# Transposing the inner activations of MLP and FFN: by TensorE, or by VectorE in 32 x 32 blocks with DMAs between partitions

## The chip, the cores and the metric

The kernel runs on one core of one Trainium2 chip. The metric is the device time of one execution in microseconds, lower is better; times of several runs are given as a median with the lowest and the highest.

The engines are named as in the profile: PE is TensorE, the matrix engine; PEld its weight loads; DVE is VectorE; ACT is ScalarE; POOL is GpSimd; SP is SyncE, whose queue issues DMAs here. An on-chip tile lies in SBUF on 128 partitions; PE writes its results to PSUM.

## What is computed

Two transformer blocks run over 256 tokens of width 1024, all in float32. The first block has four layers, each with a mixer (retention, conformer convolution, short convolution) and a squared-ReLU MLP. The second block has two layers, each with a SwiGLU FFN, a token mixing of three branches, another FFN and a gated projection (PLE). The change touches the MLPs, four of them, and the FFNs, also four:

```python
def squared_relu_mlp(x, w1, w2):
    return jnp.square(jax.nn.relu(x @ w1)) @ w2      # 1024 -> 4096 -> 1024

def _swiglu(x, w1, w3, w2):
    return (jax.nn.silu(x @ w1) * (x @ w3)) @ w2     # 1024 -> 2816 -> 1024
```

The inner activation is the argument of the second product. It comes out of the first with the tokens on the partitions, and the second needs it with the inner features on the partitions: it has to be transposed in between.

## The kernel before

**Halves.** The 256 tokens are two halves of 128. Each half is a Python generator (`first`, `second`), and `drive` (line 267) steps them in turn over one stream of weights: in each step half 0 uses unit i of the stream and half 1 unit i - 4 (`PACE`, lag 4 in the phases "1" and "A", where the MLPs and the FFNs run).

**Units.** A unit is 128 x 1024 float32 of weights (512 KB). `plan_mlp` (406) cuts an MLP into 8 groups of 512 inner features: four units of `w1`, then four of `w2`. `plan_ffn` (803) cuts an FFN into 11 groups of 256 inner features: four units "f1", each half of w1 and half of w3 and therefore loaded by two DMAs, then two units "f2". In both the first product of group g + 1 comes before the second product of group g.

**The supply.** `fill` (255) runs ahead of the step: `load_unit` (182) issues the DMA of a unit on SP into one of five raw tiles (line 189), up to eight units ahead, and `split_unit` (192) makes two tiles of it, the weights rounded to float32r by ACT (`wh`, line 204) and the remainder by DVE (`whl`, line 205), up to two units ahead, into one of eight slots. A raw tile is free when line 205 has read it; a slot is free when half 1 has used the unit (`release`, 211).

**The products.** `mm3` (306) multiplies the rounded activation with both weight tiles and the activation's remainder with the rounded weights: three matmuls for each 512 columns, so 6 for a unit and half, 12 for a unit.

**The activation.** In `mlp` (422) the first product ends in a PSUM bank; ACT applies the ReLU (434), DVE squares it (436), and the tile goes into `r[g]`. Two units later, before the second unit of the second product of the group before (`k == 1`), `tr_split` (337) transposes it: four 128 x 128 transposes on PE into a PSUM bank (`tr`, 331, recorded at line 66), and `split` (322) makes the rounded tile `t2h` by ACT (327) and the remainder `t2l` by DVE (328). These are the left-hand sides of the second product's matmuls. For group 0 that stands just ahead of its second product. In `ffn` (821) it is the same with silu (833), the product with the other half (835), tiles of 256 columns and two transposes.

**Tiles.** `B2` (109) takes a tile from one of two rings of the phase, 2 KB and 1 KB for each partition; `RINGS` gives their lengths: 30 and 6 in phase "1" (the first block), 20 and 6 in phase "A" (the FFNs). MLP tiles come from the 2 KB ring, FFN tiles of 256 columns from the 1 KB ring.

**Order.** The kernel states data dependences through tiles, and a scheduler fixes each engine's order of instructions when the program is built; waits are semaphores. Each engine and each DMA queue then works in that order.

Of the kernel before, what the change touches and what calls it, by code (L numbers as in the profile page):

```python
# [19 lines left out]
# (lag of the second half in units, splits ahead, loads ahead)  # L20
PACE = {"1": (4, 2, 8), "A": (4, 2, 8), "M": (0, 3, 6), "B": (2, 1, 6), "P": (6, 1, 8)}
# taps of the conformer's convolution that go to TensorE
# [3 lines left out]
# 2 KB slots, 1 KB slots  # L26
RM = (42, 20)
RINGS = {"1": (30, 6), "A": (20, 6), "M": RM}
# [10 lines left out]
# sets of columns of w_in, a bank each; rwkv's low ranks come with the gated delta rule's a, b and GLA's low rank  # L39
# [11 lines left out]
class Builder:  # L51
# [39 lines left out]
    # ---- phases: what fills the on-chip memory  # L91
# [16 lines left out]
    # ---- tiles  # L108
# [11 lines left out]
    def any(s, tag, shape):  # L120
        """outside the projections all four banks serve alike"""
        if s.kind == "M":
            s.turn = not s.turn
            tag = "mm" if s.turn else "tp"
        return s.bank(tag, 2, shape)
# [18 lines left out]
    def rows(s, keep, name, *vecs):  # L144
        """vectors of 128 n entries as n rows each of one tile"""
        n = sum(v.shape[0] for v in vecs)
        t = s.const.tile([n, 128], F32, tag="p " + name, name=name) if keep else s.B2((n, 128), name)
        o = 0
        for v in vecs:
            s.pin(s.nc.gpsimd.dma_start(t[o:o + v.shape[0]], v))  # L150
            o += v.shape[0]
        return t

    def columns(s, name, *rows):
        """those rows as columns"""
        n = sum(r.shape[0] for r in rows)
        t = (s.pool if s.kind == "1" else s.const).tile([128, n], F32, tag="p " + name, name=name)
        tp = s.tpb((128, n))
        o = 0
        for r in rows:  # L160
            k = r.shape[0]
            s.nc.tensor.transpose(tp[:, o:o + k], r, s.ident[0:k, 0:k])
            o += k
        s.nc.vector.tensor_copy(t, tp)
        return t

    # ---- weight stream
# [24 lines left out]
    def split_unit(s, i, early):  # L192
        """the weights as a float32r tile and the float32r rest"""
        nc = s.nc
        r, n = s.r[i], s.width[i]
        if s.plan[i][0] in EXACT:
            s.w[i] = r
            return True
        tag = s.take(s.whq, early)
        if tag is None:  # L200
            return False
        s.slot[i][1] = tag
        wh, wl = s.tile_of(tag, F32R), s.tile_of(tag, F32R, "l")
        nc.scalar.copy(wh[:, 0:n], r[:, 0:n])  # L204
        nc.vector.tensor_tensor(wl[:, 0:n], r[:, 0:n], wh[:, 0:n].bitcast(F32), op=ALU.subtract)  # L205
        s.w[i] = (wh, wl)
        s.rawq.append(s.slot[i][0])
        s.slot[i][0] = None
        return True
# [9 lines left out]
    def side_step(s, wait=True):  # L219
        """one step of the mixing that is next in turn, has what it needs and whose last step is LATENCY past"""  # L220
# [21 lines left out]
    def side_run(s):  # L242
        """what goes beside half a unit"""
# [11 lines left out]
    def fill(s, u, ahead, load, stop):  # L255
        """loads and splits that run ahead of unit u; what is for another phase takes no slot of this one's"""
# [48 lines left out]
    # ---- pieces  # L305
# [16 lines left out]
    def split(s, src):  # L322
# [4 lines left out]
        nc.scalar.copy(hh, src)  # L327
        nc.vector.tensor_tensor(ll, src, hh.bitcast(F32), op=ALU.subtract)  # L328
# [7 lines left out]

    def tr_split(s, src):
        return s.split(s.tr(src))

    def linear(s, lhs, KT, name, n=1024, out=None):  # L340
        """units of [128 K, 1024 columns]; yields the two banks"""
# [11 lines left out]
    def rstd(s, v, r=None):  # L353
        """v [128, n] already holds mean square + eps"""
# [19 lines left out]
    def times(s, x, g):  # L374
        """x g, the start of rms_norm(x, g); the scale per token is left to what follows the product"""
# [6 lines left out]
    def pre_lhs(s, x, y):  # L382
        """that transposed and split, and the scale"""
# [5 lines left out]
    def post_rms(s, ps, x, g, after):  # L389
        """x + rms_norm(ps, g), and that times the vector after"""  # L390
# [14 lines left out]
    # ---- MLP  # L405
# [16 lines left out]
    def mlp(s, h, lhs, rin):  # L422
# [4 lines left out]
        def w1(g):  # L427
# [9 lines left out]
            r[g] = a2  # L437

        yield from w1(0)
        for g in range(8):  # L440
            if g < 7:
                yield from w1(g + 1)
            at = nxt if g else [s.tr_split(r.pop(g))]
            for k in range(4):
                W = yield "w2"
                if g < 7 and k == 1:
                    nxt = [s.tr_split(r.pop(g + 1))]
# [3 lines left out]
    # ---- retention  # L451
    def ret_consts(s):
# [9 lines left out]
        for h in range(2):  # L462
# [19 lines left out]
            # columns: cos | cos | -sin | sin  # L482
# [16 lines left out]
    def rotary(s, h, ps, rin):  # L499
        """ps: two banks of 2 heads x (t1 128 | t2 128); returns transposed [128 d, 8, 128 tok] as two tiles"""  # L500
# [84 lines left out]
    # ---- conformer conv  # L585
# [23 lines left out]
    def depthwise(s, c, raws):  # L609
        """gate and convolution of channels 256 c .. 256 c + 255, both halves; DVE and TensorE share the taps"""  # L610
# [89 lines left out]
    # ---- short conv  # L700
# [51 lines left out]
    # ---- first block  # L752
# [9 lines left out]
    def layer_vec(s, key, vec, norm=False):  # L762
        """a replicated vector, loaded by the first half that asks"""
# [38 lines left out]
    # ---- second block: SwiGLU, LayerNorm, PLE  # L802
# [18 lines left out]
    def ffn(s, h, lhs):  # L821
# [4 lines left out]
        def w1(g):  # L826
# [9 lines left out]
            r[g] = b  # L836

        yield from w1(0)
        for g in range(11):
            if g < 10:  # L840
                yield from w1(g + 1)
            at = nxt if g else [s.split(s.tr(r.pop(g), 2)[:, 0:2, :])]
            for k in range(2):
                W = yield "f2"
                if g < 10 and k == 1:
                    nxt = [s.split(s.tr(r.pop(g + 1), 2)[:, 0:2, :])]
# [3 lines left out]
    def lhs(s, src, exact):  # L850
        """transposed: as it is or split"""
# [7 lines left out]
    def post_ln(s, ps, w, x, g, b):  # L859
        """x = layer_norm(alpha * x + w * ps), taken as that of x + w / alpha * ps"""  # L860
# [42 lines left out]
    # ---- second block: token mixing  # L903
# [15 lines left out]
    def mix_load(s, i):  # L919
        """the mixers' parameters of a layer, and what is fixed"""  # L920
# [76 lines left out]
    def token_mix(s, h, lhs, i):  # L997
# [7 lines left out]
        for name, cols in SETS:  # L1005
# [7 lines left out]
            if name.startswith("gate"):  # L1013
                # sigmoid(z) = (1 + tanh(z / 2)) / 2, the last half left to the end
# [19 lines left out]
    def weave(s, main, beside):  # L1034
        """main, with a step of the other after each of its own"""
# [7 lines left out]
    def inverse(s, nb, Lq, Lx, D=None):  # L1043
        """inverses of I + L (of 1 / D + L) for strictly lower triangular 64 x 64 blocks L, two above each other in each
        of nb columns of blocks; Lq(m, q) is the transposed q-th 32 x 32 diagonal block of column m, Lx(m, e) the
        transposed lower left 32 x 32 block; returns the transposed inverses, [128, nb, 64]"""
# [67 lines left out]
    def rwkv(s, h, i, q):  # L1114
# [39 lines left out]
        # sigmoid(z) = (1 + tanh(z / 2)) / 2, the halves left to what follows  # L1154
# [22 lines left out]
        # cumulative log decay inside chunks of 64, over -exp(-1/2) / 2  # L1177
# [18 lines left out]
        # kk, 2 a * kk  # L1196
# [9 lines left out]
        # decayed: [128 channels of two heads, pair, chunk (a | r), token]  # L1206
# [22 lines left out]
        def beside():  # L1229
            """what the state will need, while the inverses are on their way"""  # L1230
# [11 lines left out]
            for c in range(2):  # L1242
# [7 lines left out]
                if c == 0:  # L1250
# [5 lines left out]
                    # values, the tokens of two heads on the partitions  # L1256
# [111 lines left out]
    def softplus(s, x, w):  # L1368
        """max(x, 0) + ln(1 + exp(-|x|))"""
# [9 lines left out]
    def gdn(s, h, i, q):  # L1379
# [29 lines left out]
        # k and q side by side, two heads a tile  # L1409
# [16 lines left out]
        # columns of ss: k 0-3, q 4-7  # L1426
# [10 lines left out]
        # ln(beta / (k.k + eps))  # L1437
# [38 lines left out]
        def beside():  # L1476
            if h:
                # keys of the first half
# [41 lines left out]
        # the second chunk of 64 after the first  # L1520
# [23 lines left out]
        # rq = (q.q + eps)^-1/2 / sqrt(dk); rms over rq * O  # L1544
# [26 lines left out]
    def gla(s, h, i, q):  # L1571
# [21 lines left out]
        for b in range(2):  # L1593
            # -(z + b)
# [6 lines left out]
        # cumulative sums of -16 log a over the half  # L1601
# [9 lines left out]
        def score(kx, qx, out, n=128, keys=(0,), queries=(0,)):  # L1611
            """scores of blocks of n keys and n queries that begin at these; out(e, bank, j-th block)"""
# [15 lines left out]
        def scaled(sz):  # L1628
            """keys of the first half of each block of 2 sz, queries of the second"""
# [203 lines left out]
```

## Time and profile before

| what | us |
|---|---|
| time, median of 3 runs | 3053.36 (3052.99 to 3053.74) |
| span of the profiled execution, first to last instruction | 3051.7 |
| PE busy | 2964.7 |
| DVE busy | 1927.7 |
| ACT busy | 1521.7 |

The profile is of one execution; its page gives the span and no separate time, and it stands 1.7 us below the median of the timed runs. The mean granted clock of PE in it is 0.992.

In the rows of instruction groups the columns are line, engine, operation, output <- input with their shapes, count, then busy time in us, mean ns of one, and the idle time of the engine just before them with what ended most of it. In timelines the columns are start and duration in us, engine, line, operation, tile and count. In rows of waits they are who waited, for whom, us in total, times, longest. In rows of DMA issues they are output <- input, queue, count, KB each, and median us from issue to landing. In the rows of one tile's instructions the durations are the least, the median and the greatest in ns.

### The profile page before, as it was taken

What the parts mean: (1) busy time and instruction counts of PE and PEld (TensorE: products, weight loads), DVE (VectorE), ACT (ScalarE), POOL (GpSimd) and SP (SyncE); (2) the same over time, 40 slices, a digit from 0 to 9 for tenths busy, and PEclk for the clock granted to TensorE, in tenths of its full rate; (3) what the DMA queues carried; (4) which work ended last, traced back from release to release, by engine and by line L of the source; (5) the groups of instructions that cost most, each with busy time, mean ns of one, the idle gap of its engine ahead of it and who ended that gap; (6) DMA issues with size and microseconds to landing.
All of it is one profiled execution on the core that took longest, in us unless ns stands there. A gap on an engine that the chain in (4) does not pass through costs nothing. (4 is left out here: it accounts for less than half of the span.)

```text
span 3051.7 us, 48503 instructions
## 1 busy us (share of the span) xinstructions
PE 2964.7 (97%) x19034; PEld 2370.0 (78%) x19034; DVE 1927.7 (63%) x3039; ACT 1521.7 (50%) x2348; POOL 216.9 (7%) x349
## 2 busy tenths in 40 slices
PE   7999998999999999999999999999999999999998
PEld 5777876787878777787887787778878788777786
DVE  6566569656665666655556857565575576567556
ACT  4345454544554544544446566544444386644443
POOL 1000025000000000200000000000020000000000
PEclk9999999999999999999999999999999999999999
DMA  7456652455566655665664333466566543335663
GB/s 236 152 175 189 183 166 83 145 181 186 178 189 183 192 162 161 202 185 177 186 186 141 92 111 107 137 202 188 181 208 188 146 147 91 106 116 170 196 188 123
DMA packets 256325, 498.52 MB, mean 163 GB/s; under 512 B 24917, under 2 KB 125473, under 8 KB 256096
## 3 DMA queue, kind: packets, MB, share of 16 engines
q1 hardware_dynamic: 247424, 470.82, 50.5%
q0 software_dynamic: 8096, 22.49, 2.6%
q8 instruction: 150, 2.46, 0.3%
q10 hardware_dynamic: 576, 2.10, 0.2%
q14 instruction: 79, 0.65, 0.1%
HBM read 494.28 MB, written 1.05 MB: 162 GB/s over the span
## 5 line engine op out<-in xcount | busy, mean ns | idle before, releaser
L59 PE MATMUL acc<-wh,t2h 128*128 128x512 f32 (+1 forms) x1736 | 714.6, 413 | 16.7 <-ACT t2h L327 16.3
L205 DVE TENSOR_TENSOR whl<-raw,wh 128x1024 fp32r<-128x1024 f32 (+1 forms) x400 | 484.5, 1214 | 344.7 <-ACT wh L204 343.7
L59 PE MATMUL acc<-whl,t2h 128*128 128x512 f32 (+1 forms) x1736 | 682.6, 394 | 0.0
L204 ACT CAST wh<-raw 128x1024 fp32r<-128x1024 f32 (+1 forms) x400 | 415.8, 1042 | 459.5 <-PE acc L59 319.3
L59 PE MATMUL acc<-wh,t2l 128*128 128x512 f32 (+1 forms) x1736 | 594.4, 394 | 1.7 <-DVE t2l L328 1.6
L59 PEld LDWEIGHTS acc<-wh,t2h 128*128 128x128 f32 x1736 | 328.1, 189 | 98.1 <-ACT t2h L327 23.7
L59 PEld LDWEIGHTS acc<-wh,t2l 128*128 128x128 f32 x1736 | 326.9, 189 | 77.8 <-DVE t2l L328 5.5
L205 DVE TENSOR_TENSOR whxl<-raw,whx 128x1024 fp32r<-128x1024 f32 x213 | 260.2, 1223 | 195.9 <-ACT whx L204 195.9
L59 PEld LDWEIGHTS acc<-whl,t2h 128*128 128x128 f32 x1736 | 328.8, 189 | 62.2 <-issue 1.8
L204 ACT CAST whx<-raw 128x1024 fp32r<-128x1024 f32 x213 | 222.6, 1049 | 213.9 <-PE mm L59 130.2
L59 PE MATMUL mm<-whx,t2h 128*128 128x512 f32 x800 | 315.2, 394 | 0.6 <-ACT t2h L327 0.6
L59 PE MATMUL mm<-whx,t2l 128*128 128x512 f32 x800 | 314.4, 393 | 0.7 <-DVE t2l L328 0.7
L59 PE MATMUL mm<-whxl,t2h 128*128 128x512 f32 x800 | 313.8, 392 | 0.0
L205 DVE TENSOR_TENSOR whl<-rawx,wh 128x1024 fp32r<-128x1024 f32 x142 | 173.7, 1225 | 140.0 <-ACT wh L204 139.7
L205 DVE TENSOR_TENSOR whxl<-rawx,whx 128x1024 fp32r<-128x1024 f32 x145 | 177.1, 1222 | 129.2 <-ACT whx L204 129.2
L59 PE MATMUL acc<-whx,t2h 128*128 128x512 f32 x632 | 256.6, 406 | 1.1 <-ACT t2h L327 1.1
L59 PE MATMUL acc<-whxl,t2h 128*128 128x512 f32 x632 | 250.5, 396 | 0.0
L204 ACT CAST whx<-rawx 128x1024 fp32r<-128x1024 f32 x145 | 151.7, 1048 | 151.4 <-PE mm L59 101.4
L204 ACT CAST wh<-rawx 128x1024 fp32r<-128x1024 f32 x142 | 149.1, 1050 | 140.8 <-PE acc L59 97.2
L59 PE MATMUL acc<-whx,t2l 128*128 128x512 f32 x632 | 201.4, 395 | 0.3 <-DVE t2l L328 0.3
L327 ACT CAST t2h<-tp 128x512 fp32r<-128x512 f32 (+1 forms) x232 | 116.1, 504 | 131.1 <-PE tp L66 103.4
L59 PEld LDWEIGHTS mm<-whx,t2l 128*128 128x128 f32 x800 | 149.9, 187 | 35.3 <-DVE t2l L328 1.1
(612 smaller groups left out, 4089.7 us busy)
## 6 DMA issues: line engine op xcount, KB each, us to landing
raw<-in_mlp_w SPq DMA_DIRECT2D x153, 512.0 KB, 3.7
raw<-in_w_in SPq DMA_DIRECT2D x128, 512.0 KB, 3.6
raw<-in_ffn_w SPq DMA_DIRECT2D x222, 256.0 KB, 3.1
rawx<-in_mlp_w SPq DMA_DIRECT2D x103, 512.0 KB, 3.7
rawx<-in_ffn_w SPq DMA_DIRECT2D x130, 256.0 KB, 3.1
raw<-in_ret_w_in SPq DMA_DIRECT2D x58, 512.0 KB, 4.3
raw<-in_ffn_w SPq DMA_DIRECT2D x50, 512.0 KB, 3.7
rawx<-in_ret_w_in SPq DMA_DIRECT2D x38, 512.0 KB, 4.4
```

What stands on the lines that cost most here:

```text
L59: r = m0(out, a, b, **k)
L204: nc.scalar.copy(wh[:, 0:n], r[:, 0:n])
L205: nc.vector.tensor_tensor(wl[:, 0:n], r[:, 0:n], wh[:, 0:n].bitcast(F32), op=ALU.subtract)
L327: nc.scalar.copy(hh, src)
```

## The change

`tr_dma` takes the place of the transposes. DVE's 32 x 32 block transpose turns each block of a [128 tokens, n x 128 features] tile in place, so that block (b, c, a), of token block b and feature block a of column c, holds its features on the partitions of token block b. Sixteen DMAs then carry, for each pair (a, b), the blocks from partitions 32 b to 32 a of a second tile. A DMA moves 32 partitions with n x 32 contiguous floats each: 512 bytes in the MLP (n = 4), 256 bytes in the FFN (n = 2). They are issued on SP.

They are called where the activation is made, right after line 436 or 835, and no longer at `k == 1`; there only the split stays, and it reads `ty` in SBUF through a rearranged view, not a PSUM bank. The 1 KB ring of phase "A" grows from 6 to 12 tiles. Other transposes (the inputs of the blocks, of PLE and of the mixers) stay on PE. Comments and docstrings are removed as well.

```diff
-RINGS = {"1": (30, 6), "A": (20, 6), "M": RM}
+RINGS = {"1": (30, 6), "A": (20, 12), "M": RM}
...
     def split(s, src):
...
-        nc.scalar.copy(hh, src)
-        nc.vector.tensor_tensor(ll, src, hh.bitcast(F32), op=ALU.subtract)
+        cut = (lambda t: t.rearrange("p c (b j) -> p c b j", j=32)) if len(src.shape) == 4 else (lambda t: t)
+        nc.scalar.copy(cut(hh), src)
+        nc.vector.tensor_tensor(cut(ll), src, cut(hh.bitcast(F32)), op=ALU.subtract)
         return hh, ll
...
+    def tr_dma(s, src, n):
+        nc = s.nc
+        z = s.B2((128, 4, n, 32), "tz")
+        nc.vector.transpose(z, src.rearrange("p (c a j) -> p a c j", a=4, j=32))
+        y = s.B2((128, 4, n, 32), "ty")
+        for a in range(4):
+            for b in range(4):
+                nc.sync.dma_start(y[32 * a:32 * a + 32, b], z[32 * b:32 * b + 32, a])
+        return y.rearrange("p b c j -> p c b j")
...
     def mlp(s, h, lhs, rin):
...
-            r[g] = a2
+            r[g] = s.tr_dma(a2, 4)
...
-            at = nxt if g else [s.tr_split(r.pop(g))]
+            at = nxt if g else [s.split(r.pop(g))]
...
-                    nxt = [s.tr_split(r.pop(g + 1))]
+                    nxt = [s.split(r.pop(g + 1))]
...
     def ffn(s, h, lhs):
...
-            r[g] = b
+            r[g] = s.tr_dma(b, 2)
...
-            at = nxt if g else [s.split(s.tr(r.pop(g), 2)[:, 0:2, :])]
+            at = nxt if g else [s.split(r.pop(g))]
...
-                    nxt = [s.split(s.tr(r.pop(g + 1), 2)[:, 0:2, :])]
+                    nxt = [s.split(r.pop(g + 1))]
```

## The prediction

> **What bounds the kernel now.** I read the page's head first, then the idle times in its fifth part, then the timeline around the transposes that go, and last the queue that is to carry the new transfers.
>
> ```profile
> span 3051.7 us, 48503 instructions
> PE 2964.7 (97%) x19034; PEld 2370.0 (78%) x19034; DVE 1927.7 (63%) x3039; ACT 1521.7 (50%) x2348; POOL 216.9 (7%) x349
> L59 PE MATMUL acc<-wh,t2h 128*128 128x512 f32 (+1 forms) x1736 | 714.6, 413 | 16.7 <-ACT t2h L327 16.3
> L204 ACT CAST wh<-raw 128x1024 fp32r<-128x1024 f32 (+1 forms) x400 | 415.8, 1042 | 459.5 <-PE acc L59 319.3
> L205 DVE TENSOR_TENSOR whl<-raw,wh 128x1024 fp32r<-128x1024 f32 (+1 forms) x400 | 484.5, 1214 | 344.7 <-ACT wh L204 343.7
> SPq L189 <- DVE whl L205: 1213.8, 414, 25.4
> ```
>
> PE is busy 97% of the span, and its largest group waited only 16.7 us in the whole run. The supply chain waits backwards: the cast L204 waits for PE to give a weight tile back, the subtraction L205 waits for the cast, and the load queue (SPq) waits 1213.8 us for that subtraction to free a raw tile. So TensorE sets the pace, and whatever leaves its queue in the MLP and the FFN shortens the span, as long as the supply keeps up.
>
> **What goes.** A modelled duration is not what a transpose costs, since matmuls overlap; the starts show it.
>
> ```profile
> L66 PE MATMUL tp<-ident,relu x256: 270/272/273, 249.1 to 1422.1; 128*128 128x128 f32 x128
> 702.29 0.40 PE L59 MATMUL mm<-whx,t2l 128*128 128x512 f32 x1
> 702.52 0.60 PE L66 MATMUL tp<-ident,relu 128*128 128x128 f32 x4
> 702.88 0.48 PE L59 MATMUL acc<-wh,t2h 128*128 128x512 f32 x1
> 703.20 0.39 PE L59 MATMUL acc<-whl,t2h 128*128 128x512 f32 x1
> ...
> L66 PE MATMUL tp<-ident,glu x176: 270/271/272, 1455.3 to 3008.9; 128*128 128x128 f32 x176
> 1505.94 0.39 PE L59 MATMUL mm<-wh,t2l 128*128 128x512 f32 x1
> 1506.18 0.38 PE L66 MATMUL tp<-ident,glu 128*128 128x128 f32 x2
> 1506.31 0.48 PE L59 MATMUL acc<-whx,t2h 128*128 128x512 f32 x1
> 1506.63 0.39 PE L59 MATMUL acc<-whxl,t2h 128*128 128x512 f32 x1
> ```
>
> A matmul starts every 0.23 us. From 702.29 to 703.20 are 0.91 us, where two steps would take 0.46: four transposes cost 0.45 us. From 1505.94 to 1506.63 are 0.69 us: two cost 0.22 (with 0.232 for a step). That is 256/4 x 0.445 = 28.5 us in four MLPs and 176/2 x 0.22 = 19.4 us in four FFNs, 47.9 us in all.
>
> **What comes on VectorE and ScalarE.** The first half's tile is transposed by a STREAM_TRANSPOSE, which the kernel has elsewhere:
>
> ```profile
> L1078 DVE STREAM_TRANSPOSE invTT<-invT 128x256 f32<-128x256 f32 x20 | 8.8, 439 | 0.2
> L1078 DVE STREAM_TRANSPOSE invTT<-invT 128x128 f32<-128x128 f32 x20 | 6.2, 309 | 0.6
> L327 ACT CAST t2h<-tp 128x512 fp32r<-128x512 f32 x144 | 83.4, 586 | 101.3 <-PE tp L66 99.9 <-PE acc L59 0.7
> L327 ACT CAST t2h<-hoT 128x512 fp32r<-128x512 f32 x8 | 4.5, 616 | 0.0
> L327 ACT CAST t2h<-tp 128x256 fp32r<-128x256 f32 x88 | 32.6, 371 | 29.8 <-PE acc L59 26.3 <-PE tp L66 3.5
> L328 DVE TENSOR_TENSOR t2l<-tp,t2h 128x256 fp32r<-128x256 f32 x88 | 37.0, 420 | 9.8 <-ACT t2h L327 9.8
> ```
>
> 128 more columns cost 130 ns, so 512 take about 0.70 us. 64 x 0.70 + 88 x 0.44 = 84 us on a VectorE that is 63% busy: hidden behind matmuls. The split reads SBUF where it read PSUM: 616 ns for hoT, which lies in SBUF, is near the 586 ns of the PSUM form. Reading in runs of 32 has no row; between no change and a doubling it stays under PE's cover, and I take no change. The larger ring costs no time.
>
> **What comes on the load queue.** This is the term that decides. Each activation tile becomes 16 DMAs, and there are 64 + 88 tiles: 2432 issues, 1408 of them in the FFNs, all on SP, which also issues the weight loads in order. No row has a DMA of 32 partitions within SBUF; the nearest are SP's own loads:
>
> ```profile
> 722.63 0.33 SPq L189 DMA_DIRECT2D raw<-in_mlp_w  x1
> 759.60 0.80 SPq L189 DMA_DIRECT2D rawx<-in_sc_w_in  x2
> 1513.04 0.88 SPq L189 DMA_DIRECT2D rawx<-in_ffn_w  x2
> 1602.87 1.40 SPq L189 DMA_DIRECT2D raw<-in_w_in  x3
> L189 SPq DMA_DIRECT2D rawx<-in_ffn_w x168: 328/368/1217, 1435.1 to 2981.8; - x168
> ...
> raw<-in_ffn_w SPq DMA_DIRECT2D x222, 256.0 KB, 3.1
> raw<-in_w_in SPq DMA_DIRECT2D x8, 8.0 KB, 2.7
> raw<-in_w_in SPq DMA_DIRECT2D x8, 16.0 KB, 2.5
> ```
>
> An issue that had a wait ahead takes 0.33 us. One right behind another adds 0.80 - 0.33 = 0.47 (128 rows, one piece each). In pairs of 256 pieces it adds 0.88 - 0.37 = 0.51. In the group of three, where the second and third move only 8 and 16 KB, it adds (1.40 - 0.37)/2 = 0.51 as well: bytes do not count. From 128 to 256 pieces it grows by 0.04, so 32 pieces take off 0.03: 0.44. The ends are 0.33 and 0.51; I take **0.45**, nearest to the 0.47 row. One tile then occupies SP for 16 x 0.45 = 7.2 us.
>
> A group of the MLP (8 weight units, two halves of the tokens) needs 14.4 us of new issues and 8 loads at about 0.40, 17.6 us, against 8 x 12 x 0.232 = 22.3 us of matmuls: PE still sets the pace, and the 28.5 us come free. A group of the FFN has 6 units, four of them loaded by two DMAs:
>
> ```profile
> 1455.32 0.38 PE L66 MATMUL tp<-ident,glu 128*128 128x128 f32 x2
> 1472.53 0.38 PE L66 MATMUL tp<-ident,glu 128*128 128x128 f32 x2
> ```
>
> Its period is 17.2 us now. Its issues are 14.4 + 4 x (0.37 + 0.05 + 0.51) + 2 x 0.38 = 18.9 us: SP becomes the bound. Per FFN: 352 x 0.45 = 158.4, pairs 44 x 0.93 = 40.9, single loads 22 x 0.38 = 8.4, together 207.7 us. To this comes what SP cannot overlap: 3.1 us at the start (the first four units of one half, silu, product and transpose take 6.8 us, during which SP issues four pairs, 3.7), and 6.3 us after the last issue (landing 2.7, cast 0.37, subtraction 0.42, two units of one half 2.8). Five units stand loaded when the stage begins: -4.7. Result 212.4 us, against 11 x 17.2 = 189.3 us: **+23.1 us** per FFN, +92.4 for four. The 19.4 us of removed transposes are inside that and gain nothing.
>
> Behind a waiting issue on SP stand the weight loads, and behind a split that waits for its tile stand the casts on ScalarE. In the MLP both have cover: an activation is used some 20 us after it is made (the second product of the group before and the first of the one after, 8 units of 2.8 us, stand between), while transpose, issues, landing and split take 0.7 + 7.2 + 2.5 + 1.3 = 11.7. Only the last group of a stage has no further first-product group in between. At the FFN's end the cover is almost nothing:
>
> ```profile
> 1620.89 0.40 DVE L835 TENSOR_TENSOR glu<-silu,mm 128x256 f32<-128x256 f32 x1
> 1622.86 0.39 PE L59 MATMUL acc<-wh,t2h 128*128 128x512 f32 x1
> ```
>
> 1.6 us from the product's end to its use; that tail is in the 6.3 us above. At the MLP's end four units of 1.4 us (alone) to 2.8 us (beside the other half) stand against 11.7: 0.6 to 6.1 us are bare. I take 2 per MLP, +8 in all, since the other half mostly runs beside.
>
> **Sum:** -28.5 + 8 + 92.4 = +71.9 us on a span of 3051.7: 3123.6. The median shown is 3053.36, so 1.7 us lie around the span: **3125 us**.
>
> The DMA engines themselves are no bound:
>
> ```profile
> 205.00:400.00 195.00, 194.03 (x874) 156.50 (x874) 110.39 (x116) 94.20 (x117) 8.57 (x14) 1.00 0.62 185
> ```
>
> The last two columns are their busy share and GB/s in an MLP; a group moves 0.5 MB more in 22 us, 24 GB/s beside 185.
>
> The Trainium skill, page "DMA: Bandwidth & Descriptors", section "Rules for kernel authors", speaks against the change too, by another reason: it wants small transfers coalesced, since under 64 KB one pays mostly overhead. These are 16 and 8 KB, and the 8 KB row above lands after 2.7 us where the 256 KB loads take 3.1; the trace agrees, but by the sum it is the issue and not the landing that costs.
>
> **The rivals.**
>
> *Faster: the issues are cheap or hide.* If a 32-partition DMA costs 0.38 us (0.33 and the 0.05 between two), an FFN needs 352 x 0.38 + 49.3 (the loads) + 4.7 (both ends) = 187.8 us, 1.5 less than now: 3051.7 - 6.0 - 20.5 + 1.7 = 3026.9. With all tails covered too the whole 47.9 us come: 3005.5. It decides below 0.40 us per issue, where the FFNs lose less than the MLPs' 20.5 us. For it: the 0.33 of an issue that waited, and fewer pieces. Against: three rows of back-to-back issues at 0.47 and 0.51, whatever the bytes. The same page, section "Issuing engines are not separate DMA queues", says that the time an issue takes is usually small beside the transfer itself; by that rule the change would end at this rival's 3005.5. The trace has 0.47 beside 3.1 us for one load, which agrees for a single transfer and leaves out that 16 stand in a row.
>
> *Much slower: SP runs dry behind its own order.* After a tile's 16 issues comes the landing (2.7), the split's cast (0.37), and only then the cast and subtraction of a weight unit (1.04 + 1.21) that frees a raw tile: 5.3 us. If the order on ScalarE leaves only two units of loads to issue meanwhile (1.9), SP idles 3.4 us per tile, 88 x 3.4 = 300 us: 3425; at half of that, 3275. For it: casts and splits share one in-order queue. Against: the split of a tile stands two units behind its making, and raw tiles are loaded well ahead; the queue's waits for a landing are few:
>
> ```profile
> SPq L189 <- DMA rawx<-in_ffn_w: 5.6, 5, 2.5
> ```
>
> The upper end of the issue's price, 0.51, gives 352 x 0.06 x 4 = 84 us more: 3209.
>
> *No difference:* a price of 0.40 balances both, 3053.
>
> **How the numbers follow.** The forecast's kind, SP as the FFN's bound with a price of 0.41 to 0.51 and little extra idling: 0.58, from 3069 (at 0.41) to 3209 (at 0.51). Faster: 0.20. Within 0.2% (6 us, about what a measurement of this kernel can tell from no change): 0.05. SP running dry: 0.17. Slower in all 0.58 + 0.17 = 0.75. The range runs from 3015, which leaves out the lower part of the faster case, to 3280, which takes in half of the idling; about 0.08 and 0.11 stay outside.
>
> **What would show it.** Right: SP's issues of the new tiles stand 0.44 to 0.48 us apart; FFN groups come every 19 us or more, with PE waiting for weights or for the split, and MLP groups every 22.3 us; VectorE's transposes near 0.70 and 0.44 us with no one waiting for them. Wrong: issues under 0.40 us apart (the faster case); SP idle between tiles for landings or for VectorE, while PE waits (the dry case); or MLP groups over 23 us, which would mean that the split holds up the casts there as well.

## The result and the profile after

| kernel | median us | lowest to highest | runs |
|---|---|---|---|
| before | 3053.18 | 3052.49 to 3053.74 | 4 |
| after | 3744.95 | 3739.55 to 3748.74 | 4 |

The ratio is 1.226, 95% interval 1.2249 to 1.2278: the change costs 692 us, where the prediction had 72. First the head and three groups of the page of after.

```profile
span 3737.7 us, 51515 instructions
PE 3146.2 (84%) x18602; PEld 2434.9 (65%) x18602; DVE 2006.5 (54%) x3191; ACT 1528.3 (41%) x2348; POOL 216.2 (6%) x349
L59 PE MATMUL acc<-wh,t2h 128*128 128x512 f32 (+1 forms) x1736 | 727.3, 425 | 164.1 <-ACT t2h L328 152.9
L329 DVE TENSOR_TENSOR t2l<-ty,t2h 128x256 fp32r<-128x256 f32 (+1 forms) x152 | 81.6, 537 | 692.5 <-ACT t2h L328 672.8
L328 ACT CAST t2h<-ty 128x256 fp32r<-128x256 f32 (+1 forms) x152 | 75.1, 494 | 813.8 <-DMA ty<-tz 813.8
```

PE fell from 97% of the span to 84%. The casts of the carried tiles (L328) did not become slower themselves, but ScalarE sat idle 813.8 us ahead of them, always until the tile's DMAs had landed. The group that had waited 16.7 us now waits 164.1. PE no longer sets the pace in the MLP and the FFN. Two other views show what does. The waits of SP's queue, in a stretch of an MLP (970 to 1150 us) and then of an FFN (1720 to 1900 us); columns are who waited, for whom, us in total, times, longest:

```profile
SPq L347 <- DVE tz L343: 21.0, 10, 4.0
SPq L347 <- DMA raw<-in_mlp_w: 2.4, 3, 1.1
SPq L347 <- DMA rawx<-in_mlp_w: 1.4, 3, 0.8
```

```profile
SPq L347 <- DMA raw<-in_ffn_w: 4.7, 15, 0.7
SPq L347 <- DMA rawx<-in_ffn_w: 0.9, 4, 0.3
```

Before, SP spent most of an FFN waiting: 85.8 us of the 176 from 1455 to 1631 us for the subtraction L205 alone, and 48.1 for the activation's remainder (L328) and product (L835). In the FFN stretch of after it waits 5.6 of 180 us for loads to land and 2.3 for all else: it issues almost without a pause. The timeline of SP in an FFN shows one group of it (start and duration in us, then engine, line, operation, tile, count):

```profile
1803.67 10.01 SPq L347 DMA_DIRECT2D ty<-tz  x16
1813.78 0.53 SPq L189 DMA_DIRECT2D raw<-in_ffn_w  x1
1814.41 1.92 SPq L189 DMA_DIRECT2D rawx<-in_ffn_w  x4
1816.42 0.93 SPq L189 DMA_DIRECT2D raw<-in_ffn_w  x2
1817.45 10.69 SPq L347 DMA_DIRECT2D ty<-tz  x16
1828.25 1.55 SPq L189 DMA_DIRECT2D raw<-in_ffn_w  x3
1829.91 0.51 SPq L347 DMA_DIRECT2D ty<-tz  x1
```

From 1803.67 to 1829.91 are 26.2 us for two tiles and the ten loads of a group. Before, one half's SiLUs came 16.8 us apart through most of the stage (the 17.2 of the prediction is one of the first groups). A batch of 16 takes 10.0 us without a stop, 0.63 for each issue and not 0.45; the rest is the loads. In the MLP there are pauses. One tile there, on ScalarE, VectorE and SP (three timelines of the same stretch, in this order):

```profile
1048.84 0.62 ACT L328 CAST t2h<-ty 128x512 fp32r<-128x512 f32 x1 [7.12 <-DMA ty<-tz]
1049.36 0.68 ACT L447 ACTIVATE relu<-mm,rin 128x512 f32<-128x512 f32 x1
...
1063.11 0.62 ACT L328 CAST t2h<-ty 128x512 fp32r<-128x512 f32 x1 [6.43 <-DMA ty<-tz]
```

```profile
1050.10 0.68 DVE L449 TENSOR_TENSOR relu<-relu 128x512 f32<-128x512 f32 x1
1050.82 0.71 DVE L343 STREAM_TRANSPOSE tz<-relu 128x512 f32<-128x512 f32 x1
```

```profile
1051.59 10.01 SPq L347 DMA_DIRECT2D ty<-tz  x16
1061.70 0.53 SPq L189 DMA_DIRECT2D rawx<-in_mlp_w  x1
1062.32 1.36 SPq L189 DMA_DIRECT2D raw<-in_mlp_w  x3
1065.86 1.15 SPq L347 DMA_DIRECT2D ty<-tz  x2
```

Read them as one chain: the cast of one half's tile (1048.84), and only behind it, since ScalarE works in order, the ReLU of the other half (1049.36); the square, the block transpose, sixteen issues (to 1061.60), the landing, and the next cast at 1063.11. That is 14.3 us for a tile, 28.5 for a group. Over this stage one half's ReLUs come 29.1 us apart at the median; before it was 23.1.

Where the 686 us between the two spans lie is read from the starts of the ReLUs and SiLUs; each row has 16 or 22 of them, a stage, with the first and the last start at the end (before, after; MLP, then FFN):

```profile
L434 ACT ACTIVATE relu<-mm,rin x16: 689/690/692, 857.3 to 1020.5; 128x512 f32<-128x512 f32 x16
L833 ACT ACTIVATE silu<-mm x22: 378/384/386, 1444.1 to 1620.1; 128x256 f32<-128x256 f32 x22
```

```profile
L447 ACT ACTIVATE relu<-mm,rin x16: 681/682/690, 968.7 to 1180.6; 128x512 f32<-128x512 f32 x16
L846 ACT ACTIVATE silu<-mm x22: 373/377/384, 1667.6 to 1948.8; 128x256 f32<-128x256 f32 x22
```

An MLP's stage went from 163.2 to 211.9 us, an FFN's from 175.9 to 281.2. Summed in this way over the trace, the four MLP stages grew by 198.5 us and the four FFN stages by 419.8; the stretches behind the MLPs, up to the next stage's first such row or the end, grew by 26.1 and those behind the FFNs by 42.9; the stretch before the first lost 1.3. Together 686.0.

### The profile page after: what moved, and what is told of

It is laid out like the page before. It is cut to its first block, busy times and chain, and to the rows that moved or that the text cites. A ratio compares the mean times of both kernels' runs of the same rounds, so it can differ in the third digit from the quotient of the medians.

```text
span 3737.7 us, 51515 instructions
## 1 busy us (share of the span) xinstructions
PE 3146.2 (84%) x18602; PEld 2434.9 (65%) x18602; DVE 2006.5 (54%) x3191; ACT 1528.3 (41%) x2348; POOL 216.2 (6%) x349
## 5 line engine op out<-in xcount | busy, mean ns | idle before, releaser
L59 PE MATMUL acc<-wh,t2h 128*128 128x512 f32 (+1 forms) x1736 | 727.3, 425 | 164.1 <-ACT t2h L328 152.9
L205 DVE TENSOR_TENSOR whl<-raw,wh 128x1024 fp32r<-128x1024 f32 (+1 forms) x400 | 484.2, 1213 | 349.5 <-ACT wh L204 342.8
L59 PE MATMUL acc<-wh,t2l 128*128 128x512 f32 (+1 forms) x1736 | 612.3, 403 | 1.5 <-DVE t2l L329 1.4
L59 PEld LDWEIGHTS acc<-wh,t2h 128*128 128x128 f32 x1736 | 342.1, 198 | 271.1 <-ACT t2h L328 176.3
L329 DVE TENSOR_TENSOR t2l<-ty,t2h 128x256 fp32r<-128x256 f32 (+1 forms) x152 | 81.6, 537 | 692.5 <-ACT t2h L328 672.8
L59 PE MATMUL mm<-whx,t2h 128*128 128x512 f32 x800 | 341.0, 432 | 124.4 <-ACT whx L204 78.9
L59 PE MATMUL acc<-whx,t2h 128*128 128x512 f32 x632 | 281.1, 446 | 190.1 <-ACT t2h L328 171.8
L328 ACT CAST t2h<-ty 128x256 fp32r<-128x256 f32 (+1 forms) x152 | 75.1, 494 | 813.8 <-DMA ty<-tz 813.8
L205 DVE TENSOR_TENSOR whxl<-raw,whx 128x1024 fp32r<-128x1024 f32 x213 | 259.6, 1220 | 179.6 <-ACT whx L204 177.3
L59 PE MATMUL mm<-whxl,t2h 128*128 128x512 f32 x800 | 333.5, 422 | 2.5 <-DVE whxl L205 1.2
L59 PE MATMUL mm<-whx,t2l 128*128 128x512 f32 x800 | 329.1, 411 | 0.6 <-DVE t2l L329 0.6
L59 PEld LDWEIGHTS acc<-whx,t2h 128*128 128x128 f32 x632 | 131.7, 209 | 239.7 <-ACT t2h L328 191.5
L59 PEld LDWEIGHTS mm<-whx,t2h 128*128 128x128 f32 x800 | 160.1, 204 | 187.6 <-ACT whx L204 97.5
L59 PE MATMUL acc<-whxl,t2h 128*128 128x512 f32 x632 | 271.3, 430 | 0.1
L205 DVE TENSOR_TENSOR whxl<-rawx,whx 128x1024 fp32r<-128x1024 f32 x145 | 176.9, 1221 | 147.9 <-ACT whx L204 145.5
L205 DVE TENSOR_TENSOR whl<-rawx,wh 128x1024 fp32r<-128x1024 f32 x142 | 173.3, 1221 | 107.8 <-ACT wh L204 102.2
```

The lines of the kernel that those rows point to most:

```text
L59: r = m0(out, a, b, **k)
L328: nc.scalar.copy(cut(hh), src)
L329: nc.vector.tensor_tensor(cut(ll), src, cut(hh.bitcast(F32)), op=ALU.subtract)
```

## The experiments

All times are of the whole kernel; the kernel before took 3051.4 to 3054.3 us beside them (medians). Before, after, the runs with all 16 on POOL's queue, those through HBM, the late 8 + 8 and the last row were timed four times or more, the others once. "MLP" and "FFN" are means over the four stages of one profiled execution, measured as above. Three theories stood at first: the issue costs more because its source is SBUF; the chain through ScalarE closes on itself (batch, landing, split, the next half's activation); or SP's sum of issues alone is the bound.

| run | us | MLP | FFN |
|---|---|---|---|
| before | 3053.2 | 163.1 | 176.6 |
| after | 3745.0 | 212.8 | 281.6 |
| MLP's part only | 3279.1 | 213.7 | 176.4 |
| FFN's part only | 3512.6 | 163.2 | 280.8 |
| split of carried tiles on POOL | 3741.1 | 204.8 | 274.5 |
| all 16 on POOL's queue | 3517.3 | 212.9 | 229.3 |
| 8 on SP, 8 on POOL's queue | 3116.4 | 162.8 | 185.0 |
| 8 of double size, on SP | 3069.6 | 156.2 | 182.1 |
| through HBM, 1 + 4 on SP | 3123.3 | 167.6 | 181.6 |
| late split, 16 on SP | 3743.3 | 211.3 | 283.0 |
| late split, 16 on POOL's queue | 3200.3 | 165.3 | 194.1 |
| late split, 8 + 8 | 3117.1 | 156.2 | 184.2 |
| late split, through HBM | 3091.1 | 161.2 | 176.3 |
| 15 of 16 read HBM | 3470.8 | 184.3 | 244.8 |
| MLP groups 0 to 6 only, late split, 8 + 8 | 3030.4 | 156.7 | 176.4 |

**The price of an issue, by itself.** The kernel before with eight groups of 24 DMAs behind its end:

```diff
+        group("pmove", lambda z, y, j: nc.sync.dma_start(y[f(j % 4), j], z[f((j + 1) % 4), j % 4]))
+        group("psame", lambda z, y, j: nc.sync.dma_start(y[f(j % 4), j], z[f(j % 4), j % 4]))
+        group("psmall", lambda z, y, j: nc.sync.dma_start(y[f(j % 4), j, 0:16], z[f((j + 1) % 4), j % 4, 0:16]))
+        group("pfull", lambda z, y, j: nc.sync.dma_start(y[:, j], z[:, j % 4]))
+        group("phbm", lambda z, y, j: nc.sync.dma_start(y[f(j % 4), j], hbm[f(j), 0:128]))
+        group("phbmfull", lambda z, y, j: nc.sync.dma_start(y[:, j], hbm[128 * (j % 8):128 * (j % 8) + 128, 0:128]))
+        group("pact", lambda z, y, j: nc.scalar.dma_start(y[f(j % 4), j], z[f((j + 1) % 4), j % 4]))
+        group("ppool", lambda z, y, j: nc.gpsimd.dma_start(y[f(j % 4), j], z[f((j + 1) % 4), j % 4]))
```

> The kernel before, with eight groups of 24 DMAs each put behind its end, one group after the other: seven on SP, ACT or SP from HBM, one on POOL; the output is not touched. It measures the disputed price by itself. In the changed kernel an issue takes 588 ns and the next starts 633 ns after it, where the loads of the kernel before give 0.47. Theory 'source': the price comes from reading SBUF, so the groups pmove, psame, psmall and pfull (SBUF to SBUF; other partitions, the same partitions, 64 bytes a row, 128 partitions) lie near 0.63 us apart and phbm and phbmfull (HBM to SBUF, 32 and 128 partitions) near 0.47. Theory 'partitions': 32 partitions cost it, so pmove, psame, psmall and phbm lie near 0.63 and pfull and phbmfull near 0.47. Theory 'crossing': only transfers that change partitions cost it, so psame alone of the 32-partition groups lies near 0.47. ACT's queue (pact) is expected like SP's, POOL's (ppool) near 0.55 to 0.6 as its loads now.

The timelines of SP, ScalarE's queue and POOL in it; a row is a group (two of pmove's 24 start before the view does):

```profile
3049.73 13.88 SPq L1788 DMA_DIRECT2D pmove<-srcpmove  x22
3067.26 15.07 SPq L1789 DMA_DIRECT2D psame<-srcpsame  x24
3085.98 15.07 SPq L1790 DMA_DIRECT2D psmall<-srcpsmall  x24
3104.64 15.52 SPq L1791 DMA_DIRECT2D pfull<-srcpfull  x24
3124.32 11.02 SPq L1792 DMA_DIRECT2D phbm<-in_mlp_w  x24
3138.97 11.26 SPq L1793 DMA_DIRECT2D phbmfull<-in_mlp_w  x24
```

```profile
3154.28 15.35 ACTq L1794 DMA_DIRECT2D pact<-srcpact  x24
```

```profile
3173.85 11.79 POOL L1795 DMA_DIRECT2D ppool<-srcppool  x24 [129.47 <-DVE ppool L1777]
```

From one start to the next are, at the median, 0.633 us (pmove, psame, psmall) and 0.643 (pfull): it does not matter whether partitions are crossed, whether a row has 512 or 64 bytes, or whether 32 or 128 partitions move. It matters where the data lie: the same 32 partitions read from HBM cost 0.463, 128 of them 0.474. ScalarE's queue pays 0.641 for a read of SBUF, POOL's 0.489. So the price in after (0.63) is that of reading SBUF on this queue, and the prediction's 0.45 was that of reading HBM.

**One part alone.** The MLP's and the FFN's parts of the change, each with the other part as before (the longer ring stays). Of the MLP's part, against the kernel before, the line that makes the tile:

```diff
             nc.vector.tensor_tensor(a2, a, a, op=ALU.mult)
-            r[g] = a2
+            r[g] = s.tr_dma(a2, 4)
```

> The change in the MLPs alone; the FFNs transpose on PE as before. Theory 'chain' (the 16 issues of one tile, their landing, the split that waits for it on ACT, and behind it the other half's activation follow one another, 14.4 us for a tile against 11.55 before): 64 x 2.9 = +185 us, about 3240 us. Theory 'sum' (SP's issues alone are the bound: 32 x 0.633 + 3.3 = 23.6 us for a group against 23.1 now): +16 us, about 3070 us.

> The change in the FFNs alone; the MLPs transpose on PE as before. Theory 'chain': 13.8 us for a tile against 8.6, 88 x 5.2 = +457 us, about 3510 us. Theory 'sum': 32 x 0.633 + 4.5 = 24.8 us for a group against 17.2, with the ends +350 us, about 3400 us. With the MLP kernel its difference to before should add up to the +692 us of both, if the two stages do not touch each other.

3279.1 and 3512.6 us: 227 and 461 over before, 688 together, nearly the whole loss. So the parts hardly act on each other, and the MLP, which the prediction held to be covered, loses a third of it. Both came nearer to the figure of a chain than to the other. For the FFN that proves nothing: SP's timeline above takes 26.2 us a group with hardly a pause, near the 27.6 of two links of 13.8, so the two theories cannot be told apart by this time.

**The split away from ScalarE.** If the chain through ScalarE is what costs, the split of a carried tile on POOL frees it.

```diff
-        nc.scalar.copy(cut(hh), src)
-        nc.vector.tensor_tensor(cut(ll), src, cut(hh.bitcast(F32)), op=ALU.subtract)
+        E = (nc.gpsimd, nc.gpsimd.tensor_copy) if len(src.shape) == 4 else (nc.vector, nc.scalar.copy)
+        E[1](cut(hh), src)
+        E[0].tensor_tensor(cut(ll), src, cut(hh.bitcast(F32)), op=ALU.subtract)
```

> As changed, but the split of the carried tiles (rounded copy and remainder) runs on POOL, so that no other engine's queue stands behind the wait for the landing; SP's issues are as many as before. Theory 'chain': the link from the landing to the other half's activation is gone, SP's sum is left: MLPs +16 us, FFNs +350 us, about 3420 us. Theory 'sum': the split's place does not matter, 3745 us as changed. If PE's lower granted clock (0.924) were the cost itself, the time would stay near 3745 too unless the clock rises.

The time stayed (3741.1 us), as the theory "sum" had it; the chain's 3420 missed. The stages did become shorter, the four MLPs by 32 us and the four FFNs by 28 in all, but the stretches behind them grew by 61; why was not followed. ScalarE now waited for weights instead; the largest of these waits in this run:

```profile
ACT wh L204 <- DMA raw<-in_ffn_w: 246.2, 60, 18.4
```

And in the MLP stretch (970 to 1150 us) SP waits only 0.3 us for the block transposes, where it was 21.0, but 22.8 for loads to land, where it was 3.8: its queue has no more room. So a second bound stood right behind the first. The next eight runs vary the two things that were left: what SP has to issue, and where the split stands.

**Other queues, fewer issues.** Early split as in after. The four edits put these lines in the place of the inner statement (in the last two, of its loops too); the third puts the blocks in other places, so it keeps the bytes and not the result:

```diff
-                nc.sync.dma_start(y[32 * a:32 * a + 32, b], z[32 * b:32 * b + 32, a])
+                nc.gpsimd.dma_start(y[32 * a:32 * a + 32, b], z[32 * b:32 * b + 32, a])
...
+                (nc.sync, nc.gpsimd)[b % 2].dma_start(y[32 * a:32 * a + 32, b], z[32 * b:32 * b + 32, a])
...
+        for a in range(2):
+            for b in range(4):
+                nc.sync.dma_start(y[64 * a:64 * a + 64, b], z[64 - 64 * a:128 - 64 * a, b])
...
+        nc.sync.dma_start(d.rearrange("b p a f -> (b p) a f"), z.rearrange("p a c j -> p a (c j)"))
+        for a in range(4):
+            nc.sync.dma_start(y[32 * a:32 * a + 32].rearrange("p b c j -> p b (c j)"), d[:, :, a, :].rearrange("b p f -> p b f"))
```

where `d` is a tile in HBM.

> The 16 DMAs of a tile stand on POOL's queue, the weight loads keep SP's. Theory 'shared queue': what costs is that the weight loads stand behind each batch on SP; with their own queue PE sets the pace again, MLP groups 22.3 us, FFN groups near 17, 3000 to 3070 us in all. Rival 'loop through the engines' (issues, landing, split, next activation, each behind the other, whatever the queue): 16 x 0.489 + 1.6 + 2.7 = 12.1 us per tile, so MLP groups of 24.2 and FFN groups of some 23.5 us, near 3390 us.

> 8 of the 16 DMAs stay on SP, 8 go to POOL's queue, side by side. Shared queue: SP has 8 x 0.633 = 5.1 us per tile; MLP 2 x 5.1 + 8 loads of 0.40 = 13.4 us of 22.3, FFN 10.1 + 4.7 = 14.8 of 17.2, both covered: 3005 to 3080 us. Loop through the engines: 5.1 + 1.8 + 2.7 = 9.6 per tile, MLP covered, FFN groups 19 us, near 3100 us.

> 8 DMAs of 64 partitions in place of 16 of 32, all on SP: the same bytes, blocks put in other places, so the values of MLP and FFN differ from the reference's. If the count of issues is the price (0.633 each, whatever the partitions): SP has 5.1 us per tile as in the run with two queues, MLP 13.4 us of 22.3, FFN 14.8 of 17.2, so 3005 to 3090 us. If the price went with partitions or bytes, the batch would keep its 10 us and the time would stay near 3740.

> The tile goes to HBM with one DMA of 128 partitions and comes back with four of 32 partitions: 5 issues on SP instead of 16, 0.64 + 4 x 0.46 = 2.5 us, and the first read waits 1.6 to 2 us for the write's landing with the weight loads behind it: 4.3 us of SP per tile. Shared queue: MLP 8.6 + 3.2 of 22.3 us, FFN 8.6 + 4.7 of 17.2, both covered, so 3005 to 3060 us. Loop through the engines: 4.3 + 1.8 + 2.7 = 8.8 per tile, MLP covered and FFN groups 17.6 us, so 3020 to 3090 us.

With all 16 on POOL's queue the weight loads are alone on SP, which again waits for raw tiles most of the time (the waits of its queue):

```profile
SPq L189 <- DVE whl L205: 1419.7, 434, 36.6
```

Still the time is 3517.3 us (ratio 1.1507, 1.1466 to 1.1548), over the rival's 3390 and far from the 3000 to 3070 of a shared queue. The MLP stages stay at 212.9 us. One tile's batch after the other on POOL's queue there:

```profile
1042.54 7.39 POOL L347 DMA_DIRECT2D ty<-tz  x15 [9.62 <-issue]
...
1056.24 7.82 POOL L347 DMA_DIRECT2D ty<-tz  x16 [5.59 <-issue]
```

From start to start are 13.7 us, where the rival had 12.1, and POOL idles 5.6 of them: freed of SP, the MLP is held by the chain through ScalarE, which the late split below bears out. Half as many issues on SP bring nearly everything back: 3116.4 us with the other half on POOL's queue, 3069.6 with the same bytes in eight DMAs of double size, where the MLP is faster than before (156.2 against 163.1 us). The forecasts by SP's sum were 3005 to 3090. With two queues the other theory's 3100 came nearer, but not for its reason: it had FFN groups of 19 us, and the FFN stages stayed 5 to 8 us over those of before in all three runs, under 1 us a group. The route through HBM gives 1.022 (1.0174 to 1.0265), over both of its forecasts. The Trainium skill, page "DMA: Bandwidth & Descriptors", section "Rules for kernel authors", says that spreading DMAs over issuing engines brings no bandwidth and only saves issue time, and that small ones are to be made into one; both runs agree on the issue time, which was worth over 600 us here; that spreading brings no bandwidth no run here shows.

**The late split.** The split is asked for ahead of the fourth unit of the next first product, and no longer two units after the tile is made. An MLP's last group has no next first product; its split moves from two units after the tile to four, and that of an FFN's last group stays where it was. Parts of the edit, in the MLP:

```diff
             for k in range(0, 8, 2):
                 W = yield "w1"
+                if k == 6 and g - 1 in r and g > 1:
+                    at[0] = s.split(r.pop(g - 1))
...
-                if g < 7 and k == 1:
-                    nxt = [s.split(r.pop(g + 1))]
+                if g == 6 and k == 3:
+                    nxt = s.split(r.pop(g + 1))
```

and in the FFN in the same way.

> The split of a tile is asked for just before its last cover ends (ahead of the fourth unit of the next first product) and no longer two units after the tile is made; the 16 DMAs stay on SP. Theory 'two bounds': the split's cast, placed on ScalarE before its tile can be there, holds the weight casts; and SP's own sum, 32 x 0.633 + 10 x 0.47 = 25.0 us per FFN group against 17.2 and 20.3 + 3.8 = 24.0 per MLP group against 22.3. This edit takes the first away and leaves the second: 3053 + 44 x 7.8 + 32 x 1.7 = 3450 us (3400 to 3560). If the place of the split alone were the cause: 3005 to 3060. If SP alone: no change, 3740.

> The late split and all 16 DMAs on POOL's queue. Two bounds: both are gone (POOL issues 2 x 16 x 0.489 = 15.6 us per group of 17.2 or 22.3), so 3005 to 3050 us. If the loop through the engines holds whatever the place of the split: near 3500, as with POOL's queue alone (3517).

> The late split with 8 DMAs on SP and 8 on POOL's queue (3116 us with the early split). Two bounds: SP 10.1 + 4.7 of 17.2 us in an FFN group, the tile there 5.1 + 1.8 us after its transpose, five units before its split: 3005 to 3040 us. If the late split did not matter: 3116.

> The late split with one write to HBM and four reads back (3123 us with the early split). Two bounds: 3005 to 3040 us. If SP's waits for the write's landing were what costs (189 us of waits in that run's trace), it stays at 3100 or more.

With 16 on SP nothing moves (3743.3 us), as the theory "SP alone" had it, not the 3450 of the two bounds as I had priced them. With 16 on POOL's queue the same edit takes 317 us away (3517.3 to 3200.3), and the MLP stages fall from 212.9 to 165.3. So the split's place costs where SP does not, and where SP does, it is hidden behind SP. It does not bring the 3005 to 3050 that I expected; ScalarE still waits 267.5 us in that run for carried tiles to land, and why was not followed. SP's timeline in an MLP of the late split, and its waits from 970 to 1150 us:

```profile
1046.55 1.51 SPq L189 DMA_DIRECT2D raw<-in_mlp_w  x3
1048.15 0.42 SPq L189 DMA_DIRECT2D rawx<-in_mlp_w  x1
1048.66 11.84 SPq L347 DMA_DIRECT2D ty<-tz  x16
1060.61 0.53 SPq L189 DMA_DIRECT2D rawx<-in_mlp_w  x1
```

```profile
SPq L347 <- DMA raw<-in_mlp_w: 11.3, 12, 1.3
SPq L347 <- DMA rawx<-in_mlp_w: 8.0, 8, 1.7
SPq L347 <- DVE tz L343: 4.2, 2, 4.0
```

Loads, batch, loads, with no pause between the rows: from 1046.55 to 1060.61 are 14.1 us for a tile, and the chain of after took 14.3. The batch is 11.84 us and not 10.0, because the queue stops inside it for loads to land that it issued just before (19.3 us of this stretch); it waits for the transpose only 4.2, against 21.0 in after. The two limits lie within 0.2 us of each other here, and nothing in the runs says that they must, so each edit that took one away showed the other. The variants with few issues came out at 1.0209 (1.0195 to 1.0223) and 1.012 (1.0103 to 1.0137), over the 3005 to 3040 that I expected; 8 + 8 came out at the 3116 of its rival, in which the late split does not matter. It does matter, both ways: against the early 8 + 8 the four MLP stages are 26 us shorter and the stretches behind them 20 us longer, 24.4 over before where the early split had 4.8. Through HBM it is the same (18.6 against 2.5), and in the last version below, which leaves the stage's last group to PE, it is 9.9. So in an MLP the late split pays in the stage and costs at its end. The FFN gains nothing or loses 8 us a stage; which waits make it so was not followed further.

**The source of the reads alone.** Fifteen of a tile's sixteen DMAs read rows of a weight, so the kernel computes with other values; the number of DMAs, their bytes and their queue stay.

```diff
-                nc.sync.dma_start(y[32 * a:32 * a + 32, b], z[32 * b:32 * b + 32, a])
+                src = s.io["mlp_w1"][0, 32 * b:32 * b + 32, 32 * n * a:32 * n * (a + 1)].rearrange("p (c j) -> p c j", j=32)
+                nc.sync.dma_start(y[32 * a:32 * a + 32, b], src if a + b else z[0:32, 0])
```

> 15 of a tile's 16 DMAs read the same number of bytes from HBM (rows of a weight) in place of SBUF, so MLP and FFN work on other values; number, partitions, bytes, queue and the split's place stay. If SP's sum of issue times is the bound and the price goes by the source (0.46 from HBM against 0.63 from SBUF): 0.633 + 15 x 0.463 = 7.6 us per tile; FFN groups 15.2 + 5.2 of loads + 0.9 = 21.3 us against 26.7, FFN stages 224 us against 281, MLPs covered again (156 to 163 us against 213): 3210 to 3320 us in all. If every tile only loses its own 2.5 us from a chain through the engines: 3745 - 152 x 2.5 = 3365. If the source does not matter inside the kernel: 3740.

The rows of the tiles' instructions (least, median and greatest duration in ns), of after and then of this run, and this run's casts in an MLP:

```profile
L347 SPq DMA_DIRECT2D ty<-tz x2432: 507/588/1707, 241.0 to 3692.7; - x188
```

```profile
L348 SPq DMA_DIRECT2D ty<-in_mlp_w x2280: 310/419/1764, 237.2 to 3425.7; - x190
```

```profile
1025.46 0.62 ACT L328 CAST t2h<-ty 128x512 fp32r<-128x512 f32 x1 [4.42 <-DMA ty<-in_mlp_w]
1025.99 0.68 ACT L448 ACTIVATE relu<-mm,rin 128x512 f32<-128x512 f32 x1
...
1038.38 0.62 ACT L328 CAST t2h<-ty 128x512 fp32r<-128x512 f32 x1 [4.24 <-DMA ty<-in_mlp_w]
```

The price goes by the source inside the kernel too (0.419 against 0.588 us, with some 0.045 between two). Time falls by 274 us to 3470.8, not to 3210 to 3320, and the rival's 3365 is missed as well. The MLP was to be covered and is not: the chain through ScalarE takes 12.9 us from cast to cast (8.8 of them the batch), two of them 25.8 against 22.3 of matmuls. And in the FFN SP's queue stops longer, for loads to land above all: 3.4 us a group where I had put 0.9 (26.4 us of waits from 1600 to 1780 us, with 248 issues of tiles, 32 a group). This run has the price of the prediction (0.46 beside 0.45), and so shows what else the prediction missed.

**A version that beats both.** DMAs only where SP has room: MLP groups 0 to 6, 8 on SP and 8 on POOL's queue, the late split; the MLP's last group and the FFN as before.

```diff
-            r[g] = a2
+            r[g] = s.tr_dma(a2, 4) if g < 7 else a2
...
+                (nc.sync, nc.gpsimd)[b % 2].dma_start(y[32 * a:32 * a + 32, b], z[32 * b:32 * b + 32, a])
```

> A version meant to beat both: only the MLP's groups 0 to 6 go by DMA, 8 on SP and 8 on POOL's queue, with the late split; the MLP's last group and all of the FFN keep TensorE's transposes. SP has 10.1 + 3.8 us of a group's 22.3, so PE sets the pace and 56 of the 64 tiles' transposes go: 56 x 0.445 = 24.9 us less, 3025 to 3035 us (ratio 0.991 to 0.994). If the tails or the loads lose it again: 3050 or more.

3030.36 us (3027.07 to 3041.24, 6 runs), ratio to before 0.9927, interval 0.9913 to 0.9941: a small gain of 23 us, inside the 3025 to 3035 that was expected. The ReLUs of an MLP in its trace:

```profile
L450 ACT ACTIVATE relu<-mm,rin x16: 686/690/691, 853.6 to 1010.3; 128x512 f32<-128x512 f32 x16
```

156.7 us against 163.2: 6.5 us an MLP, 26 in four, the price of 56 tiles' transposes (24.9). In the profiled execution, one of the slower (3039.9 us), 10.4 us of them are lost again between the first MLP and the second's first ReLU (180.0 us against 169.6); why was not followed.

## Why the prediction was wrong

The sign and the place (SP's queue, the FFN first) were right; the size was 620 us too low, and the time lies far over the range. Step by step:

- **"I take 0.45, nearest to the 0.47 row"**: this step failed first. The rows were loads from HBM, and the new DMAs read SBUF: 0.633. The ends of 0.33 and 0.51 did not hold it, because the nearest rows shared the queue but not the source. "Bytes do not count" was right; the 0.03 off for fewer pieces is 0.011 in the probe. With 0.633 the prediction's own sum gives 352 x 0.633 + 49.3 + 4.7 = 276.8 us per FFN against 189.3, +350 for four, instead of +92.4. The FFN stages and what stands behind them grew by 462.7, so the price makes 258 of the 370 us that were missed there. Reading HBM at the prediction's price took 274 us off the measured time.
- **"What SP cannot overlap" only at an FFN's two ends**: too small. With reads of HBM an FFN group still takes 23.2 us (180 us by 248 / 32) and not 18.9: the tiles' issues 15.2 and not 14.4, some 3 us of stops, and about 5 for the loads where 4.5 were put. In after the group is the 26.2 of the timeline.
- **"In the MLP both have cover", 20 us against 11.7**: failed. The 20 us run to the tile's use by PE. But the split stands on ScalarE two units after the tile is made, ahead of the other half's ReLU, and ScalarE works in order: what counts is the place of the first instruction that waits, not the last use. The chain that closes through it takes 14.3 us a tile. The four MLP stages were to gain 28.5 us and grew by 198.5: 227 us missed, the second large error. The sign named for this, groups over 23 us, came; but moving the split alone would not have mended it, because SP's own line is 14.1 us a tile.
- **The tails**: 2 us per MLP were taken, the stretches behind the MLPs grew by 26.1 / 4 = 6.5.
- **The 28.5 us of the MLP** come only where SP has room: 26 in the last run. Those of the FFN gained nothing, as said.
- **VectorE's and ScalarE's part** was right: 0.711 and 0.445 us per block transpose (0.70 and 0.44 estimated). SP waits for them only as a link of the MLP's chain (21.0 of 180 us), hardly in the FFN. The landing was put too high (2.7 us, 1.8 measured). The cast from SBUF takes 0.618 us against 0.586 from PSUM, and reading in runs of 32 did not double it. These are the two rows:

```profile
L343 DVE STREAM_TRANSPOSE tz<-glu x88: 431/445/448, 1671.1 to 3682.3; 128x256 f32<-128x256 f32 x88
L343 DVE STREAM_TRANSPOSE tz<-relu x64: 702/711/715, 240.2 to 1637.7; 128x512 f32<-128x512 f32 x64
```

- **The rival "SP runs dry"** had the mechanism of the MLP, a split on ScalarE that holds the next link, and put it in the FFN, where SP waits 7.9 us of 180 in all. Its 3.4 us of idling a tile is twice what SP shows in the MLP: 21.0 us of waiting for the transpose in 180, or 1.7 for each of 12.6 tiles (180 / 14.3). The faster rival, below 0.40 us an issue, is ruled out by the probe: every group on SP lies above it, and the new tiles' at 0.633.

## What to carry to other kernels

Price a new DMA by its source as well as by its queue, and multiply before anything else: sixteen issues a tile made a queue that only loaded weights the bound of the kernel. When transfers take the place of an operation, ask where the first in-order instruction stands that waits for them and what is queued behind it; the distance to the last use is no cover. When one edit against a suspected bound shows nothing, look for a second bound of the same size before dropping the first, and change both at once.

## What the runs showed of the hardware that was not expected

An issue that reads SBUF takes 0.633 us on SP and 0.641 on ScalarE's queue, one that reads HBM 0.463 on SP; 32 or 128 partitions, 64 or 512 bytes a row change that by 0.011 at most. On POOL's queue the read of SBUF takes 0.489, less than on SP and less than the 0.55 to 0.6 expected from its loads of HBM (538 ns and more in the trace of before, in other shapes): there the order of the two sources is the other way round, as far as these unlike DMAs show. What makes the differences was not tried.

The mean granted clock of PE was 0.924 in after, against 0.992 before and 0.989 in the fastest version. It goes with the waits: in the trace of after it stands at half in 94 short stretches, 573 us together (9 and 52 us before), and in the 7 us ahead of such a stretch PE was idle 47% of the time, against 15% over the whole span. In the MLP and the FFN stretch of after it is 0.92 and 0.88, the third number from the end; the two behind it, the busy share and GB/s of the DMA engines, show that these are no bound there:

```profile
970.00:1150.00 180.00, 154.59 (x618) 119.23 (x617) 84.69 (x90) 66.10 (x77) 1.68 (x3) 0.92 0.45 148
1720.00:1900.00 180.00, 130.25 (x472) 97.69 (x471) 63.16 (x79) 51.26 (x68) 0.00 (x0) 0.88 0.44 130
```

Busy PE time reads too high by it: 3146.2 us against 2964.7 for fewer matmuls. In these stretches SP or the chain through ScalarE sets the pace and not PE; whether the lower clock costs something of its own elsewhere was not tried.
